# Two lasting accumulators of a seven-product pair, laid across two PSUM tiles instead of one

## The chip, the cores and the metric

The kernel runs on one core of a Trainium2 chip. The metric is device time in microseconds (us) of one execution, the median of several runs; a profile of one further execution gives every instruction's start and length. TensorE is written PE (its weight loads PEld), VectorE DVE, ScalarE ACT, GpSimd POOL, and SyncE SP, which issues all DMAs here.

## The reference

One layer of a hybrid encoder block on x (1024 tokens by 1024 channels, float32):

```python
hn = rms_norm(h, norm_in)
z = jnp.einsum('bsd,de->bse', hn, w_in)        # 1024 -> 4256 columns
zq, zkv, zkr, g_attn, u_pool, g_pool, g_merge = jnp.split(z, IN_SPLITS, axis=-1)
y_attn = mla_attention(zq, zkv, zkr, ...) * jax.nn.silu(g_attn)
y_pool = multiscale_pool(u_pool, pool_w, pool_scale) * jax.nn.silu(g_pool)
a = jnp.einsum('bsc,cd->bsd', y_attn, w_branch_attn)
p = jnp.einsum('bsc,cd->bsd', y_pool, w_branch_pool)
gate_a, gate_p = jnp.split(jax.nn.sigmoid(g_merge), 2, axis=-1)
merged = gate_a * a + gate_p * p
return rms_norm(h + jnp.einsum('bsd,de->bse', merged, w_out), norm_final)
```

The part around the change is the large input projection z, above all its gate and pooling columns (28 blocks of 128 columns).

## The kernel before

Every float32 operand is split into a high part and a rest (`split`: ACT makes the high part, DVE the rest), and a product is three matmuls instead of one: high by high, high by rest, rest by high. The 28 blocks of 128 columns of the gate and pooling projection are worked off as 14 **pairs** (class `Pair`). A pair is a 2 by 2 block product done with seven products in place of eight (Strassen's scheme in Winograd's form): `ORDER` lists the seven, each with a combination of weight blocks (A11, S2, S1, S3, A12, A22, S4, made by `preps`) and one of activations. A product is 12 matmuls of 128 by 128 weights onto 512 columns. Products go to three accumulators in PSUM, each of 512 float32 columns, which is one bank:

- `a` takes product 0, is copied out by ACT (`acopy(c21, a)`), and later takes product 4 on top; DVE then reads it into c11 (`tt(c11, a, ...)`).
- `c` takes product 2, is read by DVE into c22, and later takes product 6 on top; DVE reads it into c12. The names `a` and `c` are in `run`.
- `b` takes products 1, 3 and 5 and is read by DVE after each. It is a tile of its own (tag "p").

`a` and `c` are "lasting": they stay from the pair's first product to its last. Before, they are the left and the right half of one PSUM tile of 1024 columns (tag "s", `ps` in the rows, two slots), and successive pairs take the two slots in turn.

The code doesn't run in the order in which it is written. Each operation is recorded with a cost and with the boxes that it reads and writes; `Plan.order` lists them by engine with these costs and by free slots, and emits them. What an instruction then waits for is added below this, by semaphores, from the tiles that it touches. In the built program a write to a `ps` tile waits for the readers of that tile that were emitted before it, whichever half they read, and a reader waits for the writes to the tile that were emitted before it, whichever half they wrote. Each engine works its list off in order.

Beside the pairs run four small items of the pooling branch (`PoolItem`; tiles `d`, `gp`, `hi`, `lo`), two within the sixth pair and two within the tenth; each loads its input `d` from DRAM. SBUF tiles of tag "t" (45 slots) hold raw weights, operands, results and these loads, so a load waits until the last user of its slot is done. In the rows `z` is a pair's result tile, `wp` a split operand, `wr` raw weights, `win` a window sum of the pooling branch.

Of the kernel before, what the change touches and what calls it, by code (L numbers as in the profile page):

```python
# [8 lines left out]
F32 = mybir.dt.float32  # L9
# [6 lines left out]
T = 1024  # L16
# [193 lines left out]
def hybrid_block_kernel(  # L210
# [30 lines left out]
    def buf(tag, cols, dt, name):  # L241
        uid[0] += 1
        nm = f"{name}_{uid[0]}"
        pool = pp if tag in PSUM else tp
        b = Buf(lambda: pool.tile([P, cols], dt, tag=tag, bufs=SLOTS[tag], name=nm), tag)
        b.nm = name
        return View(b, 0, P, 0, cols)
# [9 lines left out]
    def t32(name):  # L257
        return buf("t", T, F32, name)
# [36 lines left out]
    def acopy(o, x):  # L295
        plan.add(
            "ACT",
            lambda: nc.scalar.copy(real(o), real(x)),  # L298
            0.8333 * x.n + (155 if psum(x) else 190),
            [x],  # L300
            [o],
        )

    def tt(o, a, b, op, eng="DVE"):
        e = nc.vector if eng == "DVE" else nc.gpsimd
        c = 1.055 * a.n + 145 if eng == "DVE" else 2.2 * a.n + 150
        port = eng == "POOL" or not (psum(a) or psum(b))
        plan.add(eng, lambda: e.tensor_tensor(real(o), real(a), real(b), op), c, [a, b], [o], port=port)  # L308
# [84 lines left out]
    class Acc:  # L393
        def __init__(self, kind):
            if kind == "s":
                t = buf("s", T, F32, "ps")
                self.halves = [t[:, :512], t[:, 512:]]
                self.spans = [(t, 0, T)]
            else:
                self.halves = [buf(c, 512, F32, "pb") for c in kind]  # L400
                self.spans = [(t, 512 * i, 512 * i + 512) for i, t in enumerate(self.halves)]
# [69 lines left out]
    lft, rgt = slice(0, 512), slice(512, T)  # L471
# [4 lines left out]
    class Item:  # L476
        def __init__(self, src, width, kt, run):
            self.src, self.width, self.run, self.kt = src, width, run, kt
            self.tag = raw_tag[0]
# [35 lines left out]
    items = []  # L515
    at = [0]

    def add(src, width, kt, run):
        items.append(Item(src, width, kt, run))
# [69 lines left out]
    for n, k in enumerate(ORDER):  # L589
# [9 lines left out]
        for a in range(0, T, step_n):  # L599
            c = slice(a, a + step_n)  # L600
# [31 lines left out]
    state = {}  # L632
# [252 lines left out]
    class Pair(Item):  # L885
# [4 lines left out]

        def __init__(self, i, posts, beside=()):
            self.i, self.posts, self.beside = i, posts, dict(beside)
            self.src = w_z[i]

        def load(self):
# [46 lines left out]
                )  # L942

        def run(self, it, tick):
            s = buf("s", T, F32, "ps")
            a, c = s[:, lft], s[:, rgt]
            o1, o2 = t32("z"), t32("z")
            c11, c12, c21, c22 = o1[:, lft], o1[:, rgt], o2[:, lft], o2[:, rgt]

            def times(o, side):  # L950
                tt(o, o, state["r"][:, side], ALU.mult)

            self.product(a, 0, True)
            acopy(c21, a)
            tick()
            b = buf("p", 512, F32, "pb")
            self.product(b, 1, True)
            tt(c12, b, c21, ALU.add)
            tick()
            self.product(c, 2, True)  # L960
            tt(c22, c, c21, ALU.add)
            tick()
            self.product(b, 3, False)
            tt(c22, b, c22, ALU.add)
            times(c22, rgt)
            tick()
            self.product(a, 4, False)
            tt(c11, a, state["r"][:, lft], ALU.mult)
            tick()
            self.product(b, 5, False)  # L970
            tt(c21, b, c21, ALU.add)
            times(c21, lft)
            self.posts[1](o2)
            tick()
            self.product(c, 6, False)
            tt(c12, c, c12, ALU.add)
            times(c12, rgt)
            self.posts[0](o1)
            tick()
# [205 lines left out]
    for h in range(HEADS):  # L1185
# [4 lines left out]
        s = heads[h % 2]  # L1190
        for qr in range(4):
            prs = []
            for i in (2 * qr, 2 * qr + 1):
                nk = 128 * (i + 1)
                ps = buf("s", T, F32, "sc")
                q = slice(128 * i, 128 * i + 128)
                n = nk if nk <= 512 else nk // 2
                ps = ps[:, 512 - n :]
# [19 lines left out]
            for g in range(qr + 1):  # L1218
                ps = buf("p", 512, F32, "pt")
# [25 lines left out]
            a = buf("oa", 256, F32, "oa")  # L1245
            r, c = (0, 64) if h % 2 == 0 else (64, 0)
# [14 lines left out]
    for i in range(8):  # L1261
# [9 lines left out]
        for n, (a, b) in enumerate(spans):  # L1271
            c = slice(a, b)
            ps = buf(tags[n], T if tags[n] == "s" else 512, F32, "po")[:, : b - a]
# [103 lines left out]
```

## Time and profile before

| | us |
|---|---|
| three runs | 719.16, 715.87, 715.16; median 715.87 |
| the profiled execution, its own time | 716.69 |
| its span, first to last instruction | 714.9 |
| PE busy | 694.6 (97%) |
| PEld busy | 580.9 (81%) |
| DVE busy | 524.3 (73%) |
| ACT busy | 319.8 (45%) |
| POOL busy | 104.7 (15%) |

The pairs take the stretch from 71 to 355 us of the span. Matmuls overlap each other: one of 512 columns is listed with 0.39 us, but in a run without waits the next one starts 0.227 us later. So PE's idle time understates a wait; the distance from start to start shows it.

### The profile page before, as it was taken

The numbers are of one execution on the slowest core, as the hardware profiler recorded it, in microseconds if no ns is written. First come the engines' busy times: TensorE is split into PE (matmuls) and PEld (weight loads), VectorE is DVE, ScalarE is ACT, GpSimd is POOL, SyncE is SP. The second block draws the span as 40 slices with busy tenths as digits, with TensorE's granted clock in tenths as the row PEclk, the third lists the DMA queues.
The fourth block names the chain that finished last, engine by engine and source line by source line (L and its number), as shares of the span: only waits on it lengthen the run. The fifth ranks groups of instructions, "written<-read, shape, count | busy, mean of one in ns | idle before, by whom it ended". The sixth has DMA issues, their size and how long they took to land.

```text
span 714.9 us, 9564 instructions
## 1 busy us (share of the span) xinstructions
PE 694.6 (97%) x3428; PEld 580.9 (81%) x3428; DVE 524.3 (73%) x823; ACT 319.8 (45%) x587; POOL 104.7 (15%) x140
## 2 busy tenths in 40 slices
PE   9999999999999999999999899999999999999996
PEld 6878887888787877887787789989998777888885
DVE  5587997777977689778869678888787859933223
ACT  5854424331332344333336567767766625321112
POOL 0020100300012030300101044445443100000000
PEclk9999999999999999999999999999999999999998
DMA  8956433122715436233867986544332489413131
GB/s 314 369 190 244 148 119 118 65 112 95 281 59 177 176 105 233 96 118 88 319 236 271 342 192 188 149 132 110 104 84 75 144 312 408 168 59 117 60 117 60
DMA packets 39567, 120.70 MB, mean 169 GB/s; under 512 B 5088, under 2 KB 6240, under 8 KB 39520
## 3 DMA queue, kind: packets, MB, share of 16 engines
q1 hardware_dynamic: 39520, 120.09, 49.3%
q8 instruction: 27, 0.44, 0.3%
q14 instruction: 20, 0.16, 0.1%
HBM read 81.14 MB, written 37.88 MB: 166 GB/s over the span
## 4 chain that ended last, share of the span: by engine, by line
PE 78%; DVE 9%; DMA 7%; issue 3%; ACT 2%; SPq 1%; DVEq 0%; ACTq 0%
PE ps L275 25%; PE pb L275 20%; PE po L275 12%; PE sc L275 7%; PE o L275 5%; PE pf L275 5%; PE pt L282 4%; DMA wr<-w_bp 2%; DVE z L308 2%; DMA d<-d_d 1%; DVE wp L308 1%; DMA go<-gate_d 1%; DMA zkv<-zkv_d 1%; ACT hi L298 1%; DVE lo L308 1%
## 5 line engine op out<-in xcount | busy, mean ns | idle before, releaser
L275 PE MATMUL pb<-t,wp 128*128 128x512 f32 x504 | 121.7, 390 | 0.0
L275 PE MATMUL ps<-xa,wp 128*128 128x512 f32 x392 | 114.1, 391 | 3.1 <-DVE z L308 2.4
L275 PEld LDWEIGHTS pb<-t,wp 128*128 128x128 f32 x504 | 94.4, 188 | 19.9 <-DVE z L308 0.3
L298 ACT CAST wp<-wr 128x512 fp32r<-128x512 f32 x98 | 58.8, 619 | 102.7 <-DVE wr L308 38.9
L275 PEld LDWEIGHTS ps<-xa,wp 128*128 128x128 f32 x392 | 73.6, 188 | 20.5 <-DVE z L308 3.7
L308 DVE TENSOR_TENSOR wp<-wr,wp 128x512 fp32r<-128x512 f32 x98 | 72.2, 753 | 9.7 <-ACT wp L298 9.6
L322 POOL TENSOR_SCALAR pr<-pr,small 128x384 f32<-128x384 f32 (+4 forms) x64 | 48.2, 758 | 71.8 <-DVE small L348 59.0
L290 ACT ACTIVATE pr<-sc,small 128x384 f32<-128x384 f32 (+4 forms) x64 | 47.7, 746 | 20.7 <-DVE small L357 19.7
L308 DVE TENSOR_TENSOR pT<-pt,pT 128x512 fp32r<-128x512 f32 (+1 forms) x80 | 48.6, 632 | 9.0 <-ACT pT L298 8.3
L357 DVE TENSOR_REDUCE small<-sc 128x1 f32<-128x128 f32 (+3 forms) x64 | 47.5, 750 | 9.4 <-PE sc L275 8.6
L308 POOL TENSOR_TENSOR z<-z,sig 128x512 f32<-128x512 f32 x16 | 23.5, 1487 | 202.5 <-ACT sig L290 200.1
L275 PE MATMUL po<-wol,hi 128*128 128x512 f32 (+1 forms) x136 | 51.2, 377 | 0.0
L275 PE MATMUL po<-woh,lo 128*128 128x512 f32 (+1 forms) x136 | 51.2, 376 | 0.0
L275 PE MATMUL po<-woh,hi 128*128 128x512 f32 (+1 forms) x136 | 51.2, 376 | 0.0
L298 ACT CAST pT<-pt 128x512 fp32r<-128x512 f32 (+1 forms) x80 | 41.2, 545 | 17.2 <-PE pt L282 16.6
L275 PE MATMUL o<-pT,v 128*128 128x256 f32 (+1 forms) x320 | 47.7, 282 | 0.6 <-DVE oa L308 0.4
L275 PEld LDWEIGHTS o<-pT,v 128*128 128x128 f32 x320 | 43.7, 189 | 3.2 <-DVE oa L308 0.8
L308 DVE TENSOR_TENSOR z<-pb,z 128x512 f32<-128x512 f32 x42 | 28.9, 687 | 23.5 <-PE pb L275 18.2
L308 DVE TENSOR_TENSOR res<-po,res 128x512 f32<-128x512 f32 (+1 forms) x17 | 11.2, 660 | 46.9 <-PE po L275 46.9
L275 PE MATMUL ps<-xb,wp 128*128 128x512 f32 x112 | 43.6, 390 | 0.0
L282 PE MATMUL pt<-ident,pr 128*128 128x128 f32 x288 | 42.2, 274 | 0.0
L275 PE MATMUL ps<-t,wp 128*128 128x512 f32 x168 | 41.4, 393 | 0.6 <-ACT z L298 0.3
(192 smaller groups left out, 1383.9 us busy)
## 6 DMA issues: line engine op xcount, KB each, us to landing
wr<-w_z SPq DMA_DIRECT2D x30, 512.0 KB, 4.9
gate_d<-z SPq DMA_DIRECT2D x16, 512.0 KB, 2.6
xt<-xr SPq DMA_DIRECT2D x8, 512.0 KB, 10.6
go<-gate_d SPq DMA_DIRECT2D x16, 256.0 KB, 2.7
mp_d<-go SPq DMA_DIRECT2D x16, 256.0 KB, 3.1
gate<-gate_d SPq DMA_DIRECT2D x8, 512.0 KB, 7.4
mp<-mp_d SPq DMA_DIRECT2D x8, 512.0 KB, 8.3
wo<-w_o SPq DMA_DIRECT2D x8, 512.0 KB, 8.7
```

The source lines that it names most:

```text
L275: nc.tensor.matmul(real(o), real(a), real(b), start=s, stop=e, **kw)
L282: nc.tensor.transpose(real(o), real(a), real(ident))
L290: nc.scalar.activation(real(o), real(x), func, scale=real(scale), **kw)
L298: lambda: nc.scalar.copy(real(o), real(x)),
L308: plan.add(eng, lambda: e.tensor_tensor(real(o), real(a), real(b), op), c, [a, b], [o], port=port)
L322: e.tensor_scalar(real(o), real(a), real(s1), real(s2), op0, op1)
L357: lambda: nc.vector.tensor_reduce(real(o), real(a), axis=AX.X, op=ALU.max, negate=True),
```

## The change

`state["acc"]` holds both "s" tiles from the first pair to the last. `a` lies in the first and `c` in the second; successive pairs take the left and the right halves in turn.

```diff
@@ -890,6 +890,7 @@
 
         def __init__(self, i, posts, beside=()):
             self.i, self.posts, self.beside = i, posts, dict(beside)
+            self.turn = len(items)
             self.src = w_z[i]
 
         def load(self):
@@ -942,8 +943,10 @@
                 )
 
         def run(self, it, tick):
-            s = buf("s", T, F32, "ps")
-            a, c = s[:, lft], s[:, rgt]
+            if "acc" not in state:
+                state["acc"] = [buf("s", T, F32, "ps") for _ in range(2)]
+            half = (lft, rgt)[self.turn % 2]
+            a, c = (v[:, half] for v in state["acc"])
             o1, o2 = t32("z"), t32("z")
             c11, c12, c21, c22 = o1[:, lft], o1[:, rgt], o2[:, lft], o2[:, rgt]
 
```

The built program has the same instructions in the same order on every engine, with the same shapes. What differs is which tile `ps` is, which slots of tag "t" some tiles get, and so the semaphores that some instructions wait for. Three places follow; the names behind `waits` are the engines (or DMA queues) whose semaphores are waited for.

On PE, the second pair's last product onto `c` (product 6); `ps_874` before is the one tile of that pair, `ps_746` now the tile of all `c`:

```order
L275 MATMUL ps_874<-xa_148,wp_940 128x512 [waits DVE_49,Activation_49]
L275 MATMUL ps_874<-xb_158,wp_940 128x512
L275 MATMUL ps_874<-xa_148,wp_940 128x512
L275 MATMUL ps_874<-xa_194,wp_940 128x512 [waits DVE_49]
L275 MATMUL ps_874<-xb_203,wp_940 128x512
L275 MATMUL ps_874<-xa_194,wp_940 128x512
```

```order
L275 MATMUL ps_746<-xa_148,wp_940 128x512 [waits DVE_49,Activation_49]
L275 MATMUL ps_746<-xb_158,wp_940 128x512
L275 MATMUL ps_746<-xa_148,wp_940 128x512
L275 MATMUL ps_746<-xa_194,wp_940 128x512
L275 MATMUL ps_746<-xb_203,wp_940 128x512
L275 MATMUL ps_746<-xa_194,wp_940 128x512
```

Nothing moved; the fourth matmul no longer waits for DVE, whose operation there is the read of `a` into c11.

On PE, the end of the sixth pair's product 6 and the seventh pair's product 2 (both onto `c`), before and now:

```order
L275 MATMUL ps_1416<-xa_263,wp_1495 128x512
L275 MATMUL ps_1504<-t_65_317,wp_1553 128x512 [waits Activation_49]
L275 MATMUL ps_1504<-t_65_317,wp_1553 128x512 x2
L275 MATMUL ps_1504<-t_89_512,wp_1553 128x512 x3
L275 MATMUL ps_1504<-t_107_618,wp_1553 128x512 x3
L275 MATMUL ps_1504<-t_127_729,wp_1553 128x512 x3
```

```order
L275 MATMUL ps_746<-xa_263,wp_1491 128x512
L275 MATMUL ps_746<-t_65_317,wp_1548 128x512 [waits Activation_49]
L275 MATMUL ps_746<-t_65_317,wp_1548 128x512
L275 MATMUL ps_746<-t_65_317,wp_1548 128x512 [waits DVE_49]
L275 MATMUL ps_746<-t_89_512,wp_1548 128x512 x3
L275 MATMUL ps_746<-t_107_618,wp_1548 128x512 x3
L275 MATMUL ps_746<-t_127_729,wp_1548 128x512 [waits DVE_49]
L275 MATMUL ps_746<-t_127_729,wp_1548 128x512 x2
```

Both pairs' `c` now lie in one tile. The tenth matmul of the seventh pair's product got a wait for DVE: the read of the sixth pair's `c` into c12, which in turn waits for the ninth matmul.

On SP, the loads for the tenth pair's two pooling items (`d` and `gp`), before and now:

```order
L377 DMA d_2039<-d_d_1489 128x1024 [waits DMAHW3_49,PE_49]
L377 DMA gp_2041<-gp_d_1810 128x1024 [waits DMAHW4_49,PE_49]
L377 DMA ga_d_2052<-z_1910 128x1024 [waits DMAHW5_49,Pool_49]
L377 DMA d_2090<-d_d_1439 128x1024 [waits DMAHW6_49,DVE_49]
L377 DMA gp_2096<-gp_d_1767 128x1024 [waits DMAHW7_49,DMAHW5_49]
```

```order
L377 DMA d_2031<-d_d_1485 128x1024 [waits DMAHW3_49,PE_49]
L377 DMA gp_2033<-gp_d_1804 128x1024 [waits DMAHW4_49,PE_49]
L377 DMA ga_d_2044<-z_1903 128x1024 [waits DMAHW5_49,Pool_49]
L377 DMA d_2082<-d_d_1435 128x1024 [waits DMAHW6_49,DVE_49,PE_49]
L377 DMA gp_2088<-gp_d_1761 128x1024 [waits DMAHW7_49,DVE_49]
```

The second `d` got another slot, the one of the tenth pair's operand A12, and so a wait for PE (the end of product 4, which reads it). Within the sixth pair it is the other way round: the second `d` there waited for a DVE split and now waits for PE's product 2 of that pair.

## Rows read from the trace of the kernel before

**Rows 1.** The page, first part: busy us (share of the span) x instructions, by engine.

```profile
PE 694.6 (97%) x3428; PEld 580.9 (81%) x3428; DVE 524.3 (73%) x823; ACT 319.8 (45%) x587; POOL 104.7 (15%) x140
```

**Rows 2.** Waits of PEld, 71 to 355 us: us in total, times, longest.

```profile
PEld ps L275 <- ACT z L298: 3.8, 6, 1.1
PEld ps L275 <- DVE z L308: 3.7, 3, 1.3
```

**Rows 3.** Chain that ended last, 71 to 355 us: start, us, what.

```profile
107.67 0.69 PE ps L275 x3
...
108.39 0.70 DVE z L308
...
109.14 2.37 PE ps L275 x9
...
246.68 2.72 PE pb L275 x12
```

**Rows 4.** The same chain, the eighth pair.

```profile
218.11 2.05 PE ps L275 x9
...
220.19 0.59 ACT z L298
...
220.82 0.98 PE ps L275 x3
...
221.83 0.70 DVE z L308
...
222.57 0.97 PE ps L275 x3
```

**Rows 5.** The same chain, the thirteenth pair.

```profile
324.81 0.69 PE ps L275 x3
...
325.58 0.70 DVE z L308
...
326.33 5.73 PE ps L275 x24
```

**Rows 6.** Timeline of PE, 296.9 to 303.2 us: start, us, instruction xcount.

```profile
297.00 2.88 PE L275 MATMUL pb<-t,wp 128*128 128x512 f32 x12
300.02 3.03 PE L275 MATMUL ps<-t,wp 128*128 128x512 f32 x12
```

**Rows 7.** Timeline, 196 to 198.5 us: DVE's read of the sixth pair's `c`.

```profile
197.01 0.68 DVE L308 TENSOR_TENSOR z<-ps,z 128x512 f32<-128x512 f32 x1
```

**Rows 8.** Timeline of PE, 191 to 201 us: the seventh pair's product 2.

```profile
195.51 2.88 PE L275 MATMUL ps<-t,wp 128*128 128x512 f32 x12
```

**Rows 9.** The chain again, the tenth pair's pooling items.

```profile
262.35 4.31 DMA d<-d_d
...
269.12 3.96 PE pb L275 x16
```

**Rows 10.** Timeline of PE, 262 to 271 us: the tenth pair's product 4 ends, an item begins.

```profile
263.19 0.39 PE L275 MATMUL ps<-xa,wp 128*128 128x512 f32 x1
...
269.12 0.74 PE L275 MATMUL pb<-lo,wh 128*128 128x512 f32 x2 [0.32 <-DVE lo L308]
```

**Rows 11.** The chain again, the sixth pair's pooling items.

```profile
167.77 0.70 DVE z L308
...
181.36 5.05 DMA d<-d_d
...
190.18 4.13 PE pb L275 x17
```

**Rows 12.** Timeline of PE, 186 to 192 us (the row left out between: four matmuls in two groups).

```profile
189.26 0.39 PE L275 MATMUL ps<-xa,wp 128*128 128x512 f32 x1
...
190.98 0.61 PE L275 MATMUL pb<-hi,wl 128*128 128x512 f32 x2
```

**Rows 13.** Timeline, 96.3 to 98 us: c12's read in the first pair, product 2 of the second.

```profile
96.68 0.68 DVE L308 TENSOR_TENSOR z<-ps,z 128x512 f32<-128x512 f32 x1
...
97.99 0.39 PE L275 MATMUL ps<-t,wp 128*128 128x512 f32 x1
```

## Prediction

> **What bounds the kernel now.** The page first: PE is busy 97% of the span, DVE 73% [rows 1]. PE is the bound, and a change that adds no work can give at most what PE stands still. The second view is the waits of PE's weight loader in the stretch of the pairs (71 to 355 us): under the tile `ps`, which holds the two lasting accumulators, it waited six times for ACT's `z` (the copy of `a` into c21) and three times for DVE's `z` (the reads into c11 and c22), 7.5 us together [rows 2]. Nearly all that PE loses in this stretch hangs on the tile that the change divides. The third view, the chain, shows what each wait costs, since its pieces follow from end to end without gaps. Its undisturbed pace is 12 matmuls in 2.72 us, 0.2267 each [rows 3].
>
> Which operation PE waits for is told by the semaphore counts of the built program. At 109.1 us the fourth matmul of product 6 onto `c` waits for DVE's read of `a`: another bank, but the same tile. That read had itself waited for the first three matmuls onto `c`. The ping-pong stands in the rows: three matmuls, 0.70 us of DVE, then the other nine [rows 3].
>
> **What the change removes.** With `a` and `c` in two tiles, no write to the one waits for a reader of the other within a pair. I worked out each wait by start and end.
>
> - Second pair: 12 matmuls from 107.67 to 109.14 + 2.37 = 111.51, so 3.84 instead of 2.72: **1.12** [rows 3].
> - Eighth pair: the ACT copy began only after product 2 onto `c` had ended, though it reads `a`; three matmuls later DVE's read of `c` held product 4 onto `a`. 15 matmuls from 218.11 to 223.54, 5.43 instead of 3.40: **2.03** [rows 4].
> - Thirteenth pair: 27 matmuls from 324.81 to 332.06, 7.25 instead of 6.12: **1.13** [rows 5].
> - Five single waits for the ACT copy (81.5, 137.5, 257.9, 280.6, 300.0 us). The last stands in the rows: the group before starts at 297.00, so the next should at 299.72 and does at 300.02, 0.30 late; its twelve then take 3.03 instead of 2.88, 0.15 more, since the first matmul after a wait is slower to be followed: 0.45 [rows 6]. In the same way the five are 0.29, 0.46, 0.58, 0.27 and 0.45: **2.05**.
>
> Together 6.33 us. The 7.5 of the loader's view is 0.13 more for each of nine waits, idle time of the loader that delays no matmul. What comes next at each place, by its row: the true waits there (product 4 for the copy of `a`, product 6 for the read of `c`, product 3 for the read of `b`) had ended 0.4 us or more before the matmul that needs them, and most were released by PE itself, so they move with it.
>
> **What it adds.** The change makes `c` of one pair and `c` of the next neighbours in a tile; the same for `a`. A pair's product 2 now waits for the former pair's read into c12. In the trace of before that read ended ahead of the product at 12 of 13 boundaries, closest at 97.36 (96.68 + 0.68) against 97.99 us [rows 13]. The exception is the sixth pair, whose reads DVE reaches late: it starts at 197.01 [rows 7], while the seventh pair's product runs from 195.51 on [rows 8]. In the changed program the read waits for the product's ninth matmul, and the tenth for the read. The ninth starts at 195.51 + 8 x 0.227 = 197.33 and ends 0.39 later, at 197.72; the read takes 0.68, two handovers 0.04 each: the tenth starts at 198.48 instead of 197.55, 0.93 late, plus 0.11 for the restart: **1.05 us**, taken. Before shows no such wait. It can't be under 0.9 while the order stands, and is 2 if DVE arrives another microsecond late.
>
> **What it moves.** No instruction changes its place on any engine, SP's queue included. But two loads of pooling inputs get other slots and with them other waits.
>
> - Sixth pair: the second `d` was issued at 181.36, when a DVE split had ended [rows 11]. Now it waits for product 2, over by 178.6 us. Behind it hang ACT's split of `d`, DVE's rest and two DVE reads for which PE waited: from 189.26 to 190.98 five matmuls take 1.72 instead of 1.13 [rows 12]. With the load two microseconds sooner that wait of **0.59** should go; bounds 0 and 0.59.
> - Tenth pair: the second `d`, issued at 262.35 [rows 9], now waits for the end of product 4, at 263.58 (263.19 + 0.39) [rows 10]; PE comes 0.58 earlier there by the removed wait, so the load goes out 0.65 later. `gp` queues behind it on SP and has time. ACT's split, DVE's rest and PE at 269.12, which already waited for that rest [rows 10], come 0.65 later. The 0.58 gained at 257.9 is then lost in front of this wait, and 0.65 more: **1.23**, taken; bounds 0.58 (the load lands as before) and 2.
>
> The sum: 6.33 + 0.59 - 1.05 - 1.23 = **4.6 us**. From the profiled execution's 716.69 us that leaves 712.1. The three runs' median, 715.87, lies 0.8 below that execution, so the forecast on it is **711.3 us**. With all bounds good it is 6.33 + 0.59 - 0.9 - 0.58 = 5.4 (710.4), with all bad 6.33 + 0 - 2 - 2 = 2.3 (713.5). Behind 355 us nothing changes but a few waits for things long over, so the lead should last to the end.
>
> The Trainium skill (Perfetto Trace Analysis, Matmuls) says that matmul groups which rotate through different PSUM banks let ACT and DVE empty one while the next is written. Before, `a` and `c` already lie in two banks, so by that rule there is no wait to win and the sum is 0. The trace disagrees: PE stands still for a reader of the other bank [rows 3 to 5].
>
> **The rivals.**
>
> - *The lead is given back.* Between 167.77 and 190.18 the chain runs through DVE and loads and not through PE [rows 11], and again up to 269.12 [rows 9]. If these pieces don't start earlier when PE does, what was won before them is lost, and what counts is the waits behind: 0.27 + 0.45 + 1.13 = 1.85, less 0 to 0.65. That is 714.0 to 714.7, say 714.4. For it: DVE has hardly a pause there. Against it: the first piece begins when PE's product has ended (DVE's `z` at 167.77), so it moves with PE.
> - *The change does nothing*: something else, due at the same moment, holds PE at the nine places (an operand's split, say). Then 715.9. Against it: the splits waited for there were done microseconds before. The Trainium skill (PSUM, PSUM bank collisions) wants engines kept apart by bank and not by address; a program that waited by bank alone would have none of these waits, and this one has them.
> - *Both loads turn out well*: the tenth pair's `d` lands in time and the sixth pair's gain is full: 5.4 to 6 won, 710.
>
> - *Slower*: the new wait across pairs. PE gains on DVE with every wait removed, and a read of c12 that had ended in time now ends after the next product's start, at which PE stands still for up to a DVE operation and a restart, 1.05 us as above. At 13 boundaries that is 13.7 us at most; less 6.3 it gives 723. It decides itself at about six such boundaries. Against it: the closest read has 0.6 us to spare, most have 1.4 to 5, and DVE's reads are released by PE itself.
>
> **How the numbers follow.** Forecast (710.4 to 713.5) 0.70, both loads well 0.03, lead given back 0.14, nothing 0.08, slower 0.05. What this measurement can tell from no change is about 0.5%, 3.6 us: faster means under 712.3. A seventh of the forecast's chance (0.10) lies above that, so faster is 0.60 + 0.03 = 0.63; same 0.10 + 0.14 + 0.08 = 0.32; slower 0.05. The range leaves out the slower case and the case of nothing, and reaches down to the good loads and up to the lead given back: 709.3 to 714.8.
>
> **What would show it.** In the profile of the changed kernel the loader's waits of `ps` for `z` should shrink from nine to one, at about 197 us less the lead so far (some 1.7), and about 1 us long. The stretches of [rows 3 to 6] should run at 2.72 us per 12 matmuls. PE's wait for DVE's `lo` in the tenth pair should grow from 0.3 us of idle time to about 1.3, and the two slow matmul pairs of [rows 12] should be gone. The last product of the pairs should end some 4.6 us earlier, and the rest of the span should be as long as before. I am wrong if PE's lead at 355 us is under 3 us, if new waits of `ps` for DVE stand at other pair boundaries, or if the lead is lost behind the pairs.

## The result and the profile after

The changed kernel takes **711.6 us** (median of 8 runs, 709.17 to 713.81) where the kernel before took 716.26 beside it (8 runs, 714.71 to 719.99): ratio **0.9927**, 95% interval 0.9900 to 0.9954. The profiled execution took 712.28 us with a span of 710.2. The forecast was 711.3, from 709.3 to 714.8. One execution of a later experiment (the turns alone) took 1412 us, twice the others, and is left out of its numbers.

The page of the changed kernel, first part, answers to [rows 1]:

```profile
PE 691.1 (97%) x3428; PEld 581.1 (82%) x3428; DVE 524.2 (74%) x823; ACT 319.7 (45%) x587; POOL 104.8 (15%) x140
```

DVE, ACT and POOL are as busy as before within 0.1 us, PE issues the same 3428 instructions, and the span is 4.7 us shorter. Waits of PE's loader, 71 to 355 us (us in total, times, longest), against [rows 2]; first a line of before that is not there, then the changed kernel:

```profile
PEld pb L275 <- DVE lo L308: 0.7, 1, 0.7
```

```profile
PEld pb L275 <- DVE lo L308: 1.5, 2, 1.0
...
PEld ps L275 <- DVE z L308: 1.2, 1, 1.2
PEld pb L275 <- ACT hi L298: 0.7, 1, 0.7
```

Nine waits under `ps` have become one. Under `pb`, the waits for a pooling input's split have grown from one to three, 0.7 to 2.2 us together. The chain of the changed kernel in the same stretch (start, us, what), against [rows 3 to 5]:

```profile
105.11 2.72 PE pb L275 x12
107.84 2.72 PE ps L275 x12
110.56 2.72 PE pb L275 x12
...
217.10 3.40 PE ps L275 x15
220.50 2.72 PE pb L275 x12
...
259.97 4.19 DMA d<-d_d
266.60 3.94 PE pb L275 x16
...
321.54 6.12 PE ps L275 x27
```

Where the chain of before ran from PE to DVE or ACT and back, PE now follows PE at 2.72 us per twelve matmuls. Two detours remain before 330 us: DVE's read at 195.64 us (the new wait, shown below) and the `d` load at 260 us. PE's timeline at the two places where something was to be lost (start, us, instructions, idle time in brackets), and DVE's at the first:

```profile
193.40 2.20 PE L275 MATMUL ps<-t,wp 128*128 128x512 f32 x9
196.38 0.97 PE L275 MATMUL ps<-t,wp 128*128 128x512 f32 x3 [0.78 <-DVE z L308]
...
265.34 0.73 PE L275 MATMUL pb<-hi,wh 128*128 128x512 f32 x2 [0.27 <-ACT hi L298]
266.60 0.73 PE L275 MATMUL pb<-lo,wh 128*128 128x512 f32 x2 [0.53 <-DVE lo L308]
```

```profile
195.64 0.69 DVE L308 TENSOR_TENSOR z<-ps,z 128x512 f32<-128x512 f32 x1 [0.69 <-PE ps L275]
```

Nine matmuls of the seventh pair's product 2 go out, DVE then reads the sixth pair's `c` in the other half of that tile, and the last three wait for the read. The start of the tenth matmul is 1.17 us behind that of the ninth, instead of 0.23.

Both programs hold the same instructions in the same order, so the clearest view is how much earlier one and the same matmul starts in the second trace. This lead changes only where a wait goes or comes:

| place (us in the trace of before) | predicted | measured |
|---|---|---|
| first 62 us (no term) | 0 | -0.45 |
| second, eighth, thirteenth pair | 1.12, 2.03, 1.13 | 1.12, 2.05, 1.13 |
| single waits at 81.5, 137.5, 257.9, 280.6, 300 | 0.29, 0.46, 0.58, 0.27, 0.45 | 0.29, 0.46, 0.58, 0.28, 0.45 |
| sixth pair's first `d`, 184 (no term) | 0 | 0.12 |
| sixth pair's second `d`, 189 to 191 | 0.59 | 0.59 |
| new wait, sixth to seventh pair | -1.05 | -1.10 |
| tenth pair's second `d` | -1.23 | -1.11 |
| last product of the pairs, 355 (no term) | 0 | -0.15 |
| lead behind it | 4.6 | 4.25 |
| lead at 589 us | 4.6 | 4.67 |

The -1.11 at the tenth pair has two parts. 0.77 us are lost at the two rows of 265.34 and 266.60 above: there ACT waits for the load and DVE for ACT. 0.34 us are lost before, at 260.46, where PE waits for the first item's `lo`. Its load had landed long since; DVE comes late, at work without a pause from 256.27 us on:

```profile
256.27 1.67 DVE L308 TENSOR_TENSOR wr<-wr 128x512 f32<-128x512 f32 x1
...
259.19 1.22 DVE L308 TENSOR_TENSOR lo<-d,hi 128x1024 fp32r<-128x1024 f32 x1
```

```profile
260.46 0.30 PEld L275 LDWEIGHTS pb<-lo,wh 128*128 128x128 f32 x2 [0.49 <-DVE lo L308]
```

### The profile page after: what moved, and what is told of

Same layout as the page of the kernel before. It is cut to its first block, busy times and chain, and to the rows that moved or that the text cites. A ratio compares the mean times of both kernels' runs of the same rounds, so it can differ in the third digit from the quotient of the medians.

```text
span 710.2 us, 9562 instructions
## 1 busy us (share of the span) xinstructions
PE 691.1 (97%) x3428; PEld 581.1 (82%) x3428; DVE 524.2 (74%) x823; ACT 319.7 (45%) x587; POOL 104.8 (15%) x140
## 4 chain that ended last, share of the span: by engine, by line
PE 83%; DMA 6%; DVE 5%; ACT 2%; issue 2%; SPq 1%; DVEq 0%; ACTq 0%
PE ps L275 28%; PE pb L275 22%; PE po L275 12%; PE sc L275 7%; PE o L275 5%; PE pf L275 5%; PE pt L282 4%; DMA wr<-w_bp 2%; DMA wr<-w_uq 1%; DMA wo<-w_o 1%; DVE lo L308 1%; SPq L377 1%; DMA x<-xT 1%; DMA wr<-w_uv 1%; DVE ra L308 1%
```

## The experiments

The theory: PE waits by whole PSUM tile, whatever half or bank is meant, and a lead won by PE stays. The rivals: the gain lies in the turns in the halves; a lead is given back in front of the next load; the last two losses lie with DVE's queue and not with the tile or the slot. Ratios are to the kernel before on the same chip.

**The turns in the halves alone.** The pairs keep the one tile each that they have before, and only change halves. To keep the instructions in order, the planner is shown the changed kernel's places (`seen`), and the built program gets others (`at`):

```diff
+LAYOUT = [
+    (1, 0, 1, 1),
+    (0, 1, 0, 0),
...
+class Placed(View):
+    def __init__(self, seen, at):
+        super().__init__(seen.buf, *seen.box)
+        self.at = at
+
+    def ap(self):
+        return self.at.ap()
...
+            x, m, y, n = LAYOUT[state["pair"]]
+            half, (left, right) = (lft, rgt)[self.turn % 2], state["acc"]
+            a = Placed(left[:, half], state["acc"][x][:, (lft, rgt)[m]])
+            c = Placed(right[:, half], state["acc"][y][:, (lft, rgt)[n]])
```

> The kernel before with one part of the change alone: a pair's a and c stay in one tile, the pairs alternate between the two tiles, but a and c change halves with every second pair. Theory (PE waits by whole tile, not by bank or half): the nine waits of the kernel before are all there again, 7 to 8 us of the loader's waits under ps, and the time is that of before, ratio 0.998 to 1.002. Rival (the taking of turns in the halves, and with it the order in which the banks are used, is what pays): it keeps most of the 4.6 us, ratio 0.993 to 0.995, and the waits are gone.

Measured: 718.67 us (nine runs), ratio 1.0013, 0.9987 to 1.0039.

> The kernel before with the turns in the halves alone, once more for its trace, since the first look at it was of an execution of twice the length, which its ten others don't share. Theory: under ps the loader waits for ACT's and DVE's z 7 to 8 us in the pairs, in the same nine places as in the kernel before, with PE never more than 0.6 us ahead. Rival: under 2 us of such waits, PE 4 us ahead at 355 us.

Measured: 714.51 us in this one run. The loader's waits in the second trace:

```profile
PEld ps L300 <- ACT z L323: 3.8, 6, 1.1
PEld ps L300 <- DVE z L333: 3.7, 3, 1.3
```

To the tenth the numbers of [rows 2]. The lead over the first trace of before is 1.8 us and not under 0.6: 0.69 of it arises in the first 8 us, 0.18 at 62 us, 0.71 at the sixth pair's `d` loads and 0.24 at the tenth pair's, none of it at one of the nine waits. The turns win nothing by themselves.

**The eighth pair alone.** The same means, with a table whose first two rows are the places of before and repeat up to the seventh pair; the eighth row divides `a` and `c`:

```diff
+LAYOUT = [
+    (1, 0, 1, 1),
+    (0, 0, 0, 1),
...
+    (1, 0, 1, 1),
+    (0, 0, 1, 1),
+    (0, 0, 0, 1),
...
```

(The rows from the ninth pair on have changed places against before.)

> The kernel before with a and c divided in the eighth pair alone; the later pairs trade tiles so that no neighbours are disturbed, and the loads have the slots that they have before. Theory: the two waits at 218 to 223.5 us vanish, PE is 2.0 us ahead from there on, and still 2.0 (1.7 to 2.3) at the last pair product and at the end, since the chain through DVE and the loads up to 269 us moves with PE; ratio 0.9972 (0.9965 to 0.998). Rival (the lead is given back in front of the tenth pair's loads): 2.0 us ahead at 224 us, under 0.7 behind 270 us, ratio 0.999 to 1.0.

Measured: 713.91 us (12 runs), ratio 0.9963, 0.9942 to 0.9985. The eighth pair's pieces in its chain, and the loader's waits from 71 to 355 us:

```profile
217.06 3.40 PE ps L300 x15
220.46 2.72 PE pb L300 x12
```

```profile
PEld ps L300 <- ACT z L323: 2.7, 5, 0.7
PEld ps L300 <- DVE z L333: 2.5, 2, 1.3
```

One wait fewer of each kind than in [rows 2]. The lead grows from 1.05 to 3.09 us between 191 and 224 us, so by 2.04; at 355 us it is 3.67, with 0.41 more won at the tenth pair's `lo`. Nothing is given back in the pairs: that rival falls. Behind them the lead goes from 3.9 to 1.4 us between 406 and 420 us, in a pause with TensorE's lower clock behind it, and is back at 3.1 by 589 us, where before waits longer. This kernel's sixth pair shows something else. Its second `d` has the slot and the wait of before, and yet 0.59 us are won at 189 to 191 us. The two `d` loads there, from issue to landing:

```profile
DMA to landing us min/median/max: 4.3/5.1/5.9
```

In the first trace of before it is 5.1, 5.5 and 6.0: the second load took 0.8 us longer there.

**The tiles crossed.** The changed kernel, but `a` of one pair lies where `c` of the pair before lies, in the other half:

```diff
-            half = (lft, rgt)[self.turn % 2]
-            a, c = (v[:, half] for v in state["acc"])
+            state["pair"] = state.get("pair", -1) + 1
+            x, m, y, n = LAYOUT[state["pair"]]
+            a, c = state["acc"][x][:, (lft, rgt)[m]], state["acc"][y][:, (lft, rgt)[n]]
```

with rows (0, 0, 1, 1) and (1, 0, 0, 1) in turn.

> The changed kernel with the two tiles traded at every pair: a of one pair lies in the tile (not in the half) where c of the pair before lies. No bank is shared that was not shared already, and the instructions keep their order. Theory (a wait is for the whole tile): at 11 to 13 pair boundaries the next pair's product 0 now waits for the read of c after product 6, three matmuls into it as in the second pair of the kernel before, 1.0 to 1.1 us each; 11 to 14 us more than the changed kernel, less the 1.05 at the sixth boundary: 721 to 725, ratio to before 1.007 to 1.013. Rival (only a shared bank costs): as the changed kernel, 711.6, ratio 0.993.

Measured: 719.13 us (10 runs), ratio 1.0030, 1.0011 to 1.0049. The loader's waits, and one boundary on PE and on DVE:

```profile
PEld ps L291 <- DVE z L324: 9.7, 8, 1.2
```

```profile
250.90 1.07 PE L291 MATMUL ps<-xa,wp 128*128 128x512 f32 x4
252.75 2.34 PE L291 MATMUL ps<-xa,wp 128*128 128x512 f32 x9 [0.79 <-DVE z L324]
```

```profile
252.00 0.69 DVE L324 TENSOR_TENSOR z<-ps,z 128x512 f32<-128x512 f32 x1 [1.98 <-PE ps L291]
```

The first three matmuls of the next pair's `a` are out, DVE reads `c`, the other nine follow. Eight such waits cost 1.1 us each by the lead, 8.9 together; less the 1.1 that the sixth boundary no longer costs, that is 7.8. From 9 to 326 us the crossed kernel falls 8.0 us behind, and most of what is left, 0.26, arises at the sixth pair's first `d` load. Mechanism and price are the theory's; the number of places was not: eight instead of 11 to 13. I had counted the waits in the program and not those whose reader is late. No bank is written and read at once here, so a rule by banks has no place for these 8 us.

**The halves fixed.** The changed kernel without its second part:

```diff
-            half = (lft, rgt)[self.turn % 2]
-            a, c = (v[:, half] for v in state["acc"])
+            a, c = (v[:, lft] for v in state["acc"])
```

> The changed kernel without turns: a always in the left half of its tile, c always in the left half of the other. The waits are by whole tile already, so the hardware has none more to keep; only the order that is laid out beforehand now knows of the read between two neighbours' c, and puts a few products of the second and seventh pair elsewhere. Theory: the tiles alone make the gain, 710.5 to 713.5, ratio 0.992 to 0.996. Rival (the turns in the halves are needed, since a half that was just read can't be written): 11 to 14 us of waits at the boundaries, 722 or more.

Measured: 718.42 us (10 runs), ratio 1.0020, 1.0001 to 1.0039. Neither expectation holds. The loader's waits, PE's timeline, and two stretches (length, PE busy (instructions), PEld, DVE, ACT, POOL, granted clock, DMA share, GB/s):

```profile
PEld pb L275 <- DVE z L308: 4.5, 2, 3.9
```

```profile
184.17 2.93 PE L275 MATMUL pb<-t,wp 128*128 128x512 f32 x6 [3.48 <-DVE z L308]
...
357.91 1.36 PE L275 MATMUL pb<-hi,wh 128*128 128x512 f32 x2 [2.72 <-DVE zkv L308]
```

```profile
184.20:187.00 2.80, 2.80 (x7) 2.23 (x8) 2.80 (x5) 1.56 (x2) 0.00 (x0) 0.50 0.15 60
187.00:190.00 3.00, 3.00 (x15) 2.44 (x14) 1.44 (x3) 1.14 (x2) 0.00 (x0) 1.00 0.00 0
```

Under `ps` nothing is waited for any more, not even at 196 us. But the order is another one. The planner now sees that the seventh pair's `a` may be written only when the sixth's is read, and moves product 0 of the seventh pair from 180 to 197 us. In its place the sixth pair's product 3 follows at once, onto a `b` that DVE has not read yet: 3.48 us of standing still, and 2.8 us at half the clock behind it. A second pause of 2.72 us stands at the end of the pairs, with the lower clock behind it too. So the halves do count, by what the planner may do and not by what PE waits for.

**The seventh pair undivided.** By a table again, which starts like the changed kernel:

```diff
+    (0, 1, 1, 1),
+    (0, 0, 0, 1),
+    (1, 1, 0, 1),
...
```

> The changed kernel, but the seventh pair's a and c lie together in the tile that held the sixth pair's a, and from the eighth pair on the two tiles have traded places. So no c of a pair meets the sixth pair's c, whose reads come late; within the seventh pair a tile is shared again, at waits that had time to spare in the kernel before. Theory: the wait at 196.4 us, 1.07 us of PE, is gone, nothing comes in its place, and PE is 1.0 to 1.1 us ahead of the changed kernel from there to the end: 710.5 where the changed kernel has 711.6, ratio to before 0.9912. Rival (DVE is simply that late, and PE waits for it a product later, or waits return within the seventh pair): the lead is given back within the pair, 711.6, ratio 0.9927.

Measured: 710.42 us (6 runs), ratio 0.9911, 0.9882 to 0.9939. PE's timeline:

```profile
192.31 2.88 PE L291 MATMUL ps<-t,wp 128*128 128x512 f32 x12
195.03 2.88 PE L291 MATMUL pb<-t,wp 128*128 128x512 f32 x12
```

Twelve matmuls in one piece. The lead over the changed kernel goes from 1.09 to 2.19 there, 1.10 won, and is 2.76 at the end of the pairs. (It starts with 1.2 from the first 8 us.) By time alone the two kernels' intervals overlap.

**Another slot for the tenth pair's `d`.** A tile gets its slot at its first write; so one column of `gp` is written ahead of the `d` load, for the second item of that pair only:

```diff
+    def claim(d, y):
+        make = d.make
+
+        def f():
+            nc.gpsimd.memset(real(y[:, :1]), 0.0)
+            return make()
+
+        d.make = f
...
+            if self.g == 3:
+                claim(self.d.buf, self.y)
             dma(self.d, d_d[self.g])
```

> The changed kernel with one more instruction: ahead of the tenth pair's second d load, GpSimd writes one column of the tile that gp will get, so that gp takes the slot that waits for product 4, and d another, free since a store that ended at 255.2 us. Theory: d is issued near 255.3 instead of 260.0, lands near 259.5, its split is done before PE needs it, and both waits of the last pooling products (0.27 and 0.53 of idle time at 265 to 267 us, with the slower start after each) go: PE 0.8 to 1.1 us further ahead behind 268 us, to the end; ratio to before 0.9914. Rival (DVE's own queue makes lo late): d comes earlier, lo does not, nothing changes, 0.9927.

Measured: 710.28 us (6 runs), ratio 0.9903, 0.9877 to 0.9929. SP's timeline, and PE's:

```profile
257.85 0.32 SPq L393 DMA_DIRECT2D d<-d_d  x1
```

```profile
267.06 0.61 PE L291 MATMUL pb<-hi,wh 128*128 128x512 f32 x2
267.51 0.62 PE L291 MATMUL pb<-lo,wh 128*128 128x512 f32 x2
```

This execution is 2.5 us behind the first trace of the changed kernel up to there, so the load goes out at 255.3 in that trace's time, 4.6 us earlier than its 259.97. Both pauses are gone, with 1.4 us won between 261 and 268 us. That is more than expected, because the idle times of 0.27 and 0.53 us understated the waits: from start to start they were 0.43 and 0.69 too long, and 0.11 more followed each.

The edit does a second thing that was not meant. GpSimd's write waits for its slot, and behind it GpSimd's two multiplications of `z` start later, by 3.8 us in the changed kernel's time. First the changed kernel, then this one, then DVE in this one:

```profile
254.40 3.00 POOL L308 TENSOR_TENSOR z<-z,sig 128x512 f32<-128x512 f32 x2 [2.38 <-issue]
```

```profile
260.62 0.10 POOL L1061 MEMSET gp<- 128x1 f32 x1 [6.08 <-DVE wp L324]
260.71 3.38 POOL L324 TENSOR_TENSOR z<-z,sig 128x512 f32<-128x512 f32 x2
```

```profile
258.54 0.69 DVE L324 TENSOR_TENSOR wr<-wr 128x512 f32<-128x512 f32 x1
```

DVE's `wr` operation, which in the changed kernel runs beside them and takes 1.67 us, takes 0.69 here, and the `wp` before it 0.69 instead of 0.95. The first item's `lo` starts 1.2 us earlier, and the 0.34 us lost at 260.46 come back as well. So 1.4 us are the load's, and 0.34 are not.

**Both edits.**

> The changed kernel with both edits: the seventh pair undivided, and the tenth pair's d load in another slot. Theory: the two places are independent, since a lead won at one stays; 1.05 and 0.8 to 1.1 add up to 1.9 to 2.1 us, 709.6 where the changed kernel has 711.6, ratio to before 0.990 (0.9885 to 0.9915). Rival: one of the two is lost in the other, 710.6.

Measured: 710.62 us (6 runs), ratio 0.9909, 0.9879 to 0.9938. In the pairs the loader waits for no ACT, DVE or DMA any more, and PE's lead over the changed kernel grows by 1.1 at the first place and by 1.7 at the second (0.34 and 1.4 as above); from 8 us to 355 us it is 3.2. The time shows none of this beside either edit alone. Two more runs set it beside the changed kernel.

> The changed kernel once more, as the measure for the kernel with both edits: ratio to before 0.9927 within its interval. Its trace should have the same waits in the pairs as the first one, with the wait at 196 us 1.07 us long, but the 0.5 us in the first 8 us may come out otherwise.

Measured: 711.70 us (10 runs), ratio 0.9944, 0.9919 to 0.9970. The trace has the wait of the first trace's 196 us again, 1.17 us from start to start; by 8.6 us it is 1.37 ahead of that trace. But it has a wait that the first has not, at the sixth pair's first `d` load, and 1.1 us of the lead go there. PE's timeline, and the time that the two `d` loads took:

```profile
182.10 1.65 PE L275 MATMUL pb<-t,wp 128*128 128x512 f32 x6 [0.85 <-DVE z L308]
```

```profile
DMA to landing us min/median/max: 6.3/6.7/7.0
```

The first load took 7.0 us, 5.9 in the first trace.

> The kernel with both edits once more, beside the changed kernel on one chip. The traces of the two edits add up to 2.5 us of PE's lead in the pairs (1.07 at 196 us, 1.4 at 261 to 268 us), so the theory expects it 2 to 3 us below the changed kernel's median of the same call. Rival: the lead is lost behind the pairs, no difference.

Measured: 710.17 us (7 runs), ratio 0.9912, 0.9877 to 0.9947: 1.5 us below the changed kernel's median, less than the 2 to 3 expected, and within the intervals. The lead over that kernel is 3.4 us at 588 us and 0.3 at 600. PE's timeline of the kernel with both edits, and a stretch of it (length, PE busy, granted clock, DMA share, GB/s); then the changed kernel at the same matmuls:

```profile
592.82 1.20 PE L291 MATMUL ps<-hi,wl 128*128 128x512 f32 x2 [1.96 <-DVE wl L324]
...
596.34 0.62 PE L291 MATMUL ps<-hi,wh 128*128 128x512 f32 x2
```

```profile
593.40:595.90 2.50, 2.50 (x7) 0.50 1.02 402
```

```profile
594.68 0.73 PE L275 MATMUL ps<-hi,wl 128*128 128x512 f32 x2 [0.38 <-DVE wl L308]
```

```profile
595.00:597.50 2.50, 2.50 (x12) 1.00 1.02 406
```

Here the DMA engines are full (share 1.02), weights' splits hang on their loads, and who comes earlier waits longer: 1.6 us of the lead go into the wait. Behind it the granted clock is 0.50, 1.2 GHz, until the pace is back at 596.34, and the rest goes there. The first trace of the kernel with both edits has such a stretch too, at 582 to 585 us, behind a pause of 2.15 us from start to start.

**The kernel before again.**

> The kernel before once more, for a second trace of it. Theory: the nine waits of PE for a reader of the other half of its tile are at the same places and of the same length within 0.1 us, since semaphores set them. The two parts of the lead that no wait of the kernel sets, 0.5 us in the first 8 us and the 0.59 at 189 to 191 us, where a d load took 5.06 us from issue to landing, may differ: with a load of 4.3 us, as in the kernel with the eighth pair alone divided, the slow matmul pairs there are gone though the slot is the same.

Measured: 719.15 us in this one run. The nine waits are there to the tenth of a microsecond (3.8 us, 6 times, and 3.7, 3 times). The sixth pair's `d` loads came out otherwise again:

```profile
DMA to landing us min/median/max: 5.0/5.9/6.8
```

Here the first one is late too, by 0.8 us; DVE's split comes later, and PE stands still 0.65 us at 184.4, for a `b` that DVE reads behind it. The lead falls by 0.79 there. PE comes later from there on, so at 189 to 191 us nothing is left to lose: the 0.59 of the first trace come back, though the second load took 5.0 us.

## Why the prediction was right

- **The nine waits (6.33 us).** Measured 6.36, each within 0.02 of its term. That it is the tile is shown from both sides: dividing one pair removes exactly that pair's two waits, and putting neighbours' accumulators into one tile brings eight new ones of 1.1 us at halves and banks that nothing else touches. The Trainium skill (PSUM — Partial Sum Buffer, PSUM bank collisions raise a hardware error) asks that two engines don't touch one bank at a time; these runs show that a program whose waits go by tile gains nothing from a bank of its own.
- **The new wait (1.05 us).** Measured 1.10, at the tenth matmul as worked out; it goes when the seventh pair's `c` lies elsewhere.
- **The tenth pair's `d` (1.23 us).** Measured 1.11, by a path that the prediction had in part. It put the whole loss in front of one wait for the second item's `lo`, with about 1.3 us of idle time. Of the 0.58 gained at 257.9 us, 0.34 were lost at the first item's `lo` already, and that is DVE's queue: the edit of the load's slot brings them back only by moving GpSimd's work out of DVE's way. The other 0.77 are lost in two waits that end with the second load, and these are the slot's, as the prediction said.
- **The sixth pair's `d` (0.59 us).** The size came out (0.59), the reason in part. With the new slot nothing is lost at 189 to 191 us in any of seven traces, though the second load takes 5.1 to 6.3 us there. But with the old slot it is lost in one of four only: not when the second load takes 4.3 or 4.0 us (the eighth pair alone, the turns alone), and not in the second trace of before (5.0 us), where PE had already stood still at 184.4. That there was 0.59 to win hung on the execution that I read, and there I was lucky. Against a late first load the earlier issue of the second does nothing. Against the first trace of before, 0.8 us went at 184.4 in its second; with the new slot, against the first trace of the changed kernel, 1.1 went at that place in its second and 0.9 with the other slot. In these three the first load took 6.8 to 7.0 us. The mean gain of this step is not settled by these runs.
- **A lead stays.** Shown within the pairs by the eighth pair alone. Behind them it holds for the changed kernel (4.25 at 355, 4.67 at 589 us), not as a rule: the kernel with both edits lost 3 us of its lead in the stretch full of loads. My sentence that the rest runs as long as before was luck in part.
- **What no term covered.** The first 8 us vary by up to 1.4 us between executions of the same program, with the pause in front of one matmul that waits for its first operands (1.81 us in the first trace of the changed kernel, under 0.3 in the second). Up to 62 us this cost the profiled execution 0.45, and 0.15 went at 355 us; so the lead there is 4.25 and not 4.86, the sum of the steps measured between. That the median came within 0.3 us of the forecast is therefore better than the sum deserves: parts of this size fall differently in each execution and happened to cancel.

The rival that ended slower did not happen, but its mechanism is real: with the crossed tiles it strikes at eight boundaries, and the kernel is slower than before.

## What to carry to other kernels

Before two lasting accumulators are placed, list for each write which readers of the *whole tile* are still due then, those of the neighbouring group too; put together what is read long before the other is written. Read the slots of the loads anew after any such change, since they move without a line of the diff. And where loads fill the DMA engines further on, a lead won earlier buys a longer wait there: look at that stretch before adding up gains.

## What the runs showed of the hardware that was not expected

TensorE's granted clock fell to the lower of its two levels (1.2 GHz) behind single pauses of PE: after 3.87 and 3.11 us from one matmul's start to the next in the kernel with fixed halves, 2.35 and 2.15 in the two traces of the kernel with both edits, 2.20 in the one with the eighth pair alone, 2.06 in the second trace of before, 2.00 in the one with the other slot. Matmuls of 512 columns then followed each other at 0.43 us instead of 0.227 for some 3 us; with both edits, with the eighth pair alone and in before this took some 1.6 us of the lead each time. Not every such pause has it: one of 2.37 us at 415 us with the crossed tiles and one of 2.00 at 388 us with the undivided seventh pair left the clock as it was, as did all the pauses of the first traces of before and after, the longest of them 1.84. The Trainium skill (TensorE: Matmul & The Clock Gate, Part 1: The HAM clock gate) has the lower level after idle time; the traces agree that it follows a pause, and show by the numbers above that pauses of one length have it in one execution and not in another. So a lead that lengthens a later pause can cost more than the pause. A part of the spread of 713 to 721 us over the runs of before will come from this, which is argued here and not shown.

Some of DVE's operations took longer beside GpSimd's: the same `wr` operation of 128 by 512 took 1.67 us while GpSimd worked on `z` (the changed kernel, first trace) and 0.69 where GpSimd's work had moved away (the other slot). Why is not shown.
